# A third seven-product pair in the even gate/up blocks, and an order between the sums of weights and the first split of sums

## The chip, the core and the metric

The kernel runs on one core of one Trainium2 chip, in one launch. The metric is the device time of that launch in microseconds; lower is better. The engines are called as the profile calls them: PE is TensorE's matmul, PEld its weight load, DVE is VectorE, ACT is ScalarE, POOL is GpSimd, SP is SyncE, whose queue issues the loads of the weights.

## The reference

One decoder layer in float32 on 256 tokens of width 2048: a half-weighted SwiGLU feed-forward, a mixer (gated linear attention beside dilated attention, between one input and one output projection), and a second half-weighted SwiGLU feed-forward.

```python
D_MODEL = 2048; SEQ = 256; D_FF = 5632; FFN_RESIDUAL_WEIGHT = 0.5
...
def swiglu(x, w_gate, w_up, w_down):
    return (jax.nn.silu(x @ w_gate) * (x @ w_up)) @ w_down
...
x = x + FFN_RESIDUAL_WEIGHT * swiglu(rms_norm(x, ffn1_norm[l]), ffn1_w_gate[l], ffn1_w_up[l], ffn1_w_down[l])
h = rms_norm(x, mix_norm[l])
z = h @ w_in[l]
...
x = x + jnp.concatenate([o_g, o_a], axis=-1) @ w_out[l]
x = x + FFN_RESIDUAL_WEIGHT * swiglu(rms_norm(x, ffn2_norm[l]), ffn2_w_gate[l], ffn2_w_up[l], ffn2_w_down[l])
```

The change touches the gate and up products of both feed-forwards (2048 to 5632, twice), and through a shared helper the down product and the output projection.

## The kernel before

**Products.** Float32 operands are split into a high and a low part (`split`, lines 113 to 116: ScalarE copies the high part in the matmul type, VectorE subtracts it from the source), and a product takes three matmuls: high by high, weight-low by high, weight-high by low (`products`, lines 273 to 283). Activations are split once and stay in SBUF; weights are loaded and split as they are needed.

**Weights.** A load on SP's queue (line 221) brings one k-pair, 256 rows of k by two column groups of 512, 1 MB, into a raw buffer; there are three. The raw buffer holds four blocks of 512 columns. A plain pair is split in two parts, each 128 by 1,024, into a `wh` and a `wl` tile; there are four of each. `weights()` hands these parts to the matmuls in order and prepares the parts that come two later. A raw buffer is loaded again when the last instruction that reads it is done, a `wh`/`wl` pair is written again when the last matmul that reads it is done.

**Seven products.** A k-pair over both token halves and both column groups is a 2 by 2 by 2 block product: eight products of blocks, 24 matmuls. A "seven" pair takes seven products of sums of blocks (Strassen's way), 21 matmuls (`seven_products`, lines 293 to 317). The sums of activations are made once for the three pairs that can be sevens (`seven_forms`; `forms` holds pairs 0, 1 and 2 in both feed-forwards' gate/up stage). The sums of weights are made for every such pair on VectorE in `seven`, part "plain": line 243 writes two sums of 1,024 columns together, line 244 a third of 512, line 247 the fourth of 512 out of the third. Four parts go to the matmuls: "plain" (two blocks of the raw buffer), "last" (one block), "sums" (the first two sums), "more" (the third and fourth). In the gate/up stage the sums lie in a room of their own in `xs`, so the raw buffer is free after the splits of "plain" and "last" and line 247; in the down stage and the output projection the third and fourth sum are written back into the raw buffer.

**Gate/up blocks.** Each feed-forward has 11 blocks of 512 columns of gate and 512 of up, eight k-pairs each. `FF_ORDERS` (line 46) writes out their order; `g` is a seven, `s` a plain pair. Block 0 is all plain; blocks 1, 3, 5, 7 and 9 are `ssgsggss`, blocks 2, 4, 6, 8 and 10 `ssgssgss`. `seven_pair` runs a block: four banks collect the plain products and four more the products that belong to several outputs; after the last seven `fold` (lines 488 to 493) brings these to VectorE's side, and `evac` (lines 451 to 473) adds them, applies the silu gate and sends the result through transposes and moves on POOL's queue.

**Down stage.** `DOWN_ORDERS` (line 47) has sevens as well, with the same `seven`.

**Order.** The kernel is traced as a program; a planner then orders each engine's queue by a simulated time, taking what is ready and, among that, what is earlier in the program. Each engine works its queue strictly in that order on the chip. So an instruction whose operand comes later than planned holds up what stands behind it. `tc.issue_after(ins)` puts each instruction that is traced inside it on `ins`'s engine behind `ins` in that engine's order; on other engines it has no effect.

Of the kernel before, what the change touches and what calls it, by code (L numbers as in the profile page):

```python
# [28 lines left out]
EPS = 1e-6  # L29
WBUF = 4  # L30
FF_SEVEN = range(1, 11)
FF_THREE = range(1, 10, 2)
TAIL = 4
WARM = 10
GH, GDK, GDV, RANK = 4, 128, 256, 16
# [4 lines left out]
def _order(text):  # L40

    seven, plain = iter(range(text.count("g"))), iter(range(text.count("g"), len(text)))
    return [(next(seven), True) if c == "g" else (next(plain), False) for c in text]


FF_ORDERS = [_order("ssgsggss" if b in FF_THREE else "ssgssgss" if b in FF_SEVEN else "ssssssss") for b in range(FF // 512)]
DOWN_ORDERS = [_order("ssssssgssgssgsgsgsgsss"), _order("sgsgsgsgsgsgsgssgsssss")]
# [3 lines left out]
def layer_kernel(tc, x, xT, gains, gla_gate_up, gla_gate_bias, gla_out_norm, att_q_norm, att_k_norm,  # L51
                 w_ff1, w_dn1, w_mix, w_low, w_out, w_ff2, w_dn2, c_sq, c_rope, c_mask, out):

    nc = tc.nc
# [3 lines left out]
    with ExitStack() as es:  # L58
# [54 lines left out]
        def split(dst_h, dst_l, src):  # L113

            nc.scalar.activation(dst_h, src, AF.Copy)  # L115
            nc.vector.tensor_sub(dst_l, src, dst_h.bitcast(F32))  # L116
# [71 lines left out]

        AHEAD = 2
        ready = []  # L190
        raws = [None]
        started = []

        def wtile(name):
            return wp.tile([P, 2, 512], F32R, name=name, tag=name, bufs=WBUF)

        def prepare():
# [15 lines left out]
            if k in ("last", "sums", "more"):  # L213
                return seven(k, w)
# [7 lines left out]
            if k == "plain":  # L222
                return seven(k, w)
# [11 lines left out]
        def seven(part, w):  # L235

            raw = raws[0].bitcast(F32)
            room = rooms["gate" if w is w_ff1 or w is w_ff2 else "down"]
            blocks = raw.rearrange("p k j f -> p (k j) f")
            more = room.get("more", blocks[:, 0::3, :])  # L240
            if part == "plain":
                b1 = blocks[:, 0, :].unsqueeze(1).to_broadcast([P, 2, 512])
                nc.vector.tensor_add(room["sum"], b1, blocks[:, 1:3, :])  # L243
                nc.vector.tensor_add(more[:, 0, :], room["sum"][:, 0, :], blocks[:, 2, :])
                if "more" not in room:
                    split(room["wh"][:, 0, :], room["wl"][:, 0, :], blocks[:, 3, :])
                nc.vector.tensor_add(more[:, 1, :], more[:, 0, :], blocks[:, 3, :])  # L247
                wh, wl = wtile("wh"), wtile("wl")
                split(wh, wl, blocks[:, 1:3, :])
            elif part == "last":  # L250
                wh, wl = room["wh"], room["wl"]
                if "more" in room:
                    split(wh[:, 0, :], wl[:, 0, :], blocks[:, 3, :])
            else:
                wh, wl = wtile("wh"), wtile("wl")
                split(wh, wl, room["sum"] if part == "sums" else more)
            ready.append((wh, wl))

        def weights(early=False):
# [740 lines left out]
```

## Time and profile before

| | us |
|---|---|
| median of 3 runs | 1711.49 |
| lowest, highest | 1710.02, 1712.36 |
| the profiled execution, its own time | 1710.49 |
| its span, first to last instruction | 1708.7 |
| gate/up of feed-forward 1 | about 6 to 448 |
| its down stage | about 448 to 650 |
| mixer and output projection | about 650 to 1050 |
| feed-forward 2 | about 1050 to the end |

The profile is of one execution. Times in its rows count from the first instruction. A row of a group gives its count, its busy time and mean, then the idle time of its engine just before it and what ended that; a row of the timeline gives start, length, engine, line, what is written and read, shape, count, and in brackets the idle time before it with what ended it. Records of matmuls are longer than the distance between two of them, because matmuls are pipelined.

### The profile page before, as it was taken

The page shows a single profiled execution, that of the slowest core. Times are in us where ns is not written, and L with a number is a line of the kernel's source. Part 1 is how long each engine was busy: PE and PEld are TensorE (multiplying, and loading weights), DVE is VectorE, ACT ScalarE, POOL GpSimd, SP SyncE. Part 2 cuts the span into 40 slices and gives each one's busy share as a digit, 9 for nine tenths or more (in the row PEclk, how much of TensorE's full clock was granted, in tenths as well). Part 3 has the DMA queues.
Part 4 walks back from the last instruction along what each step waited for, and adds up shares of the span by engine and source line. Part 5 has one row for each costly group of instructions (what it writes and reads, how often), then busy time and mean ns, then how long its engine had stood idle before and what let it go on. Part 6 is the DMA issues. An engine that isn't in the chain of part 4 may idle for free.

```text
span 1708.7 us, 22402 instructions
## 1 busy us (share of the span) xinstructions
PE 1696.9 (99%) x7932; PEld 1477.4 (86%) x7932; DVE 1472.8 (86%) x1823; ACT 973.4 (57%) x1207; POOL 506.2 (30%) x1002
## 2 busy tenths in 40 slices
PE   9999999999999999999999999999999999999999
PEld 7888888888888878888888888888888888888887
DVE  6989999999899997577856688989998999899986
ACT  7656565555555555564654555556555655555553
POOL 0333334343400601064250034333333333420000
PEclk9999999999999999999999999999999999999999
DMA  8566656666666666567564457666666666666663
GB/s 347 211 232 225 218 210 236 212 235 216 235 245 223 216 220 226 195 231 243 190 217 169 151 198 249 231 234 210 235 224 229 223 215 219 222 247 232 220 235 135
DMA packets 85809, 378.63 MB, mean 222 GB/s; under 512 B 21393, under 2 KB 38801, under 8 KB 42689
## 3 DMA queue, kind: packets, MB, share of 16 engines
q1 hardware_dynamic: 50864, 350.25, 57.9%
q0 software_dynamic: 34112, 25.88, 5.4%
q8 instruction: 62, 1.02, 0.2%
q10 hardware_dynamic: 720, 1.07, 0.2%
q14 instruction: 51, 0.41, 0.1%
HBM read 354.57 MB, written 4.19 MB: 210 GB/s over the span
## 4 chain that ended last, share of the span: by engine, by line
PE 89%; DVE 5%; DMA 4%; issue 1%; POOL 0%; ACT 0%; DVEq 0%; SPq 0%; ACTq 0%; POOLq 0%
PE acc L281 19%; PE acc L283 19%; PE acc L279 19%; PE acc L305 5%; PE acc L306 5%; PE acc L304 5%; PE tp L283 4%; PE tp L281 4%; PE tp L279 4%; DVE wl L116 3%; DMA raw<-in_w_dn_dram 2%; PE tp L306 1%; PE tp L305 1%; PE tp L304 1%; DMA xs<-us 1%
## 5 line engine op out<-in xcount | busy, mean ns | idle before, releaser
L115 ACT ACTIVATE wh<-raw 128x1024 fp32r<-128x1024 f32 (+2 forms) x610 | 631.9, 1047 | 444.0 <-PE acc L283 207.0
L116 DVE TENSOR_TENSOR wl<-raw,wh 128x1024 fp32r<-128x1024 f32 (+1 forms) x608 | 733.1, 1215 | 127.0 <-ACT wh L115 124.3
L137 POOL DMA_DIRECT2D xs<-us x704 | 344.5, 497 | 545.6 <-DVE us L130 284.1
L283 PE MATMUL acc<-wh,hl 128*128 128x512 f32 x1192 | 359.3, 381 | 0.0
L281 PE MATMUL acc<-wl,hh 128*128 128x512 f32 x1192 | 358.8, 381 | 0.1
L279 PE MATMUL acc<-wh,hh 128*128 128x512 f32 x1192 | 347.9, 381 | 2.3 <-ACT wh L115 2.3
L279 PEld LDWEIGHTS acc<-wh,hh 128*128 128x128 f32 x1192 | 224.8, 189 | 35.4 <-ACT wh L115 3.5
L281 PEld LDWEIGHTS acc<-wl,hh 128*128 128x128 f32 x1192 | 225.1, 189 | 32.7 <-DVE wl L116 0.5
L283 PEld LDWEIGHTS acc<-wh,hl 128*128 128x128 f32 x1192 | 225.3, 189 | 32.2 <-issue 0.5
L115 ACT ACTIVATE wh<-xs 128x1024 fp32r<-128x1024 f32 x100 | 105.6, 1056 | 103.3 <-DVE xs L247 31.9
L116 DVE TENSOR_TENSOR wl<-xs,wh 128x1024 fp32r<-128x1024 f32 x100 | 120.4, 1214 | 2.7 <-ACT wh L115 2.6
L281 PE MATMUL acc<-wl,uh 128*128 128x512 f32 x368 | 113.1, 381 | 2.6 <-DVE wl L116 2.6
L283 PE MATMUL acc<-wh,ul 128*128 128x512 f32 x368 | 112.2, 379 | 0.0
L279 PE MATMUL acc<-wh,uh 128*128 128x512 f32 x368 | 106.2, 380 | 0.5 <-ACT wh L115 0.5
L137 POOL DMA_DIRECT2D hh<-us x128 | 62.1, 500 | 121.1 <-DVE xs L531 68.5
L243 DVE TENSOR_TENSOR xs<-raw 128x1024 f32<-128x1024 f32 x50 | 61.1, 1222 | 29.3 <-DMA raw<-in_w_ff_dram 29.2
L281 PEld LDWEIGHTS acc<-wl,uh 128*128 128x128 f32 x368 | 68.7, 189 | 15.1 <-DVE wl L116 5.6
L279 PEld LDWEIGHTS acc<-wh,uh 128*128 128x128 f32 x368 | 69.3, 189 | 11.1 <-ACT wh L115 1.3
L283 PEld LDWEIGHTS acc<-wh,ul 128*128 128x128 f32 x368 | 69.6, 189 | 9.9
L279 PE MATMUL tp<-wh,hh 128*128 128x512 f32 x200 | 61.6, 379 | 0.0
L281 PE MATMUL tp<-wl,hh 128*128 128x512 f32 x200 | 59.5, 379 | 0.0
L283 PE MATMUL tp<-wh,hl 128*128 128x512 f32 x200 | 59.5, 379 | 0.0
(326 smaller groups left out, 2540.0 us busy)
## 6 DMA issues: line engine op xcount, KB each, us to landing
raw<-in_w_ff_dram SPq DMA_DIRECT2D x175, 1024.0 KB, 5.1
raw<-in_w_dn_dram SPq DMA_DIRECT2D x88, 1024.0 KB, 4.9
raw<-in_w_mix_dram SPq DMA_DIRECT2D x48, 1024.0 KB, 5.0
raw<-in_w_out_dram SPq DMA_DIRECT2D x16, 1024.0 KB, 4.8
xs<-us POOLq DMA_DIRECT2D x704, 16.0 KB, 4.0
xs<-in_x_dram SPq DMA_DIRECT2D x2, 1024.0 KB, 9.5
xs<-in_x_dram POOLq DMA_DIRECT2D x2, 1024.0 KB, 5.9
hh<-us POOLq DMA_DIRECT2D x128, 16.0 KB, 3.7
```

Source lines behind the costliest of these rows:

```text
L115: nc.scalar.activation(dst_h, src, AF.Copy)
L116: nc.vector.tensor_sub(dst_l, src, dst_h.bitcast(F32))
L137: nc.gpsimd.dma_start(dst[32 * q:32 * q + 32, ..., r * n:(r + 1) * n], src[32 * r:32 * r + 32, ..., q * n:(q + 1) * n])
L243: nc.vector.tensor_add(room["sum"], b1, blocks[:, 1:3, :])
L279: nc.tensor.matmul(ps[j], lhsT=sh, rhs=alt(wh[:, j, :]), start=first and i == 0, stop=False)
L281: nc.tensor.matmul(ps[j], lhsT=sh, rhs=alt(wl[:, j, :]), start=False, stop=False)
L283: nc.tensor.matmul(ps[j], lhsT=sl, rhs=alt(wh[:, j, :]), start=False, stop=last and i == len(ws) - 1)
L304: nc.tensor.matmul(bank, lhsT=a[0], rhs=alt(ws[0][:, j, :]), start=start, stop=False)
L305: nc.tensor.matmul(bank, lhsT=a[0], rhs=alt(ws[1][:, j, :]), start=False, stop=False)
L306: nc.tensor.matmul(bank, lhsT=a[1], rhs=alt(ws[0][:, j, :]), start=False, stop=stop)
```

## The change

The list of blocks with three sevens goes from 1, 3, 5, 7, 9 to 1 to 9, so blocks 2, 4, 6 and 8 also take `ssgsggss`; block 10 keeps two. The instruction of line 247 is kept in `raws[1]`, and the split of the parts "sums" and "more" is traced inside `tc.issue_after` of it. Its subtract on VectorE then stands behind line 247 in VectorE's order; its copy on ScalarE is not bound. "more" reads what line 247 writes and comes after it in any case; "sums" does not.

```diff
 FF_SEVEN = range(1, 11)
-FF_THREE = range(1, 10, 2)
+FF_THREE = range(1, 10)
...
-        raws = [None]
+        raws = [None, None]
...
-                nc.vector.tensor_add(more[:, 1, :], more[:, 0, :], blocks[:, 3, :])
+                raws[1] = nc.vector.tensor_add(more[:, 1, :], more[:, 0, :], blocks[:, 3, :])
                 wh, wl = wtile("wh"), wtile("wl")
                 split(wh, wl, blocks[:, 1:3, :])
...
             else:
                 wh, wl = wtile("wh"), wtile("wl")
-                split(wh, wl, room["sum"] if part == "sums" else more)
+                with tc.issue_after(raws[1].ins):
+                    split(wh, wl, room["sum"] if part == "sums" else more)
             ready.append((wh, wl))
```

## The prediction

> **What bounds the kernel now.** The page's first part comes first, then a few pieces of the chain of work that ended last.
>
> ```profile
> span 1708.7 us, 22402 instructions
> PE 1696.9 (99%) x7932; PEld 1477.4 (86%) x7932; DVE 1472.8 (86%) x1823; ACT 973.4 (57%) x1207; POOL 506.2 (30%) x1002
> ```
> ```profile
> 110.78 0.86 PE acc L279 x4
> 111.64 0.22 PE acc L281
> ```
>
> TensorE is busy for all but 12 us, and four 512-column matmuls follow each other in 0.86 us, 0.215 us each. A matmul less is 0.215 us less, as long as TensorE's operands keep coming. Who delivers them shows in busy time by window, each from the first seven's `L243` of one gate/up block to that of the next (window, length, then busy us and count of PE, PEld, DVE, ACT, POOL, then clock, DMA share, GB/s). The windows are blocks 3 to 6.
>
> ```profile
> 128.53:168.00 39.47, 39.47 (x184) 34.59 (x183) 39.01 (x44) 24.56 (x28) 15.65 (x32) 1.00 0.64 223
> 168.00:208.40 40.40, 40.40 (x188) 35.16 (x187) 35.30 (x40) 22.07 (x26) 15.66 (x32) 1.00 0.66 225
> 208.40:248.00 39.60, 39.60 (x185) 34.69 (x184) 39.02 (x44) 24.68 (x28) 15.65 (x32) 1.00 0.63 224
> 248.00:288.00 40.00, 40.00 (x187) 35.01 (x187) 35.29 (x39) 22.02 (x25) 15.65 (x32) 1.00 0.65 226
> ```
>
> TensorE has no hole in any of them. VectorE alternates: 39.0 us of work in the 39.5 us of a block with three sevens, 35.3 us in one with two. The change makes every window of blocks 2 to 9 one of the first kind. So the stage moves from "TensorE alone" to "both engines, 0.45 us apart", and the question is what VectorE loses at the seams.
>
> **The reserve.** How far VectorE runs ahead is the distance from the end of a split's subtract to the first matmul that reads its `wl`. The first two rows are the full distance, just before block 3 (VectorE, then TensorE); the other two the tightest place of block 3, the last sums of its third seven.
>
> ```profile
> 126.79 1.23 DVE L116 TENSOR_TENSOR wl<-raw,wh 128x1024 fp32r<-128x1024 f32 x1 [0.76 <-ACT wh L115]
> 133.71 0.59 PE L281 MATMUL acc<-wl,hh 128*128 128x512 f32 x2
> ...
> 157.21 1.22 DVE L116 TENSOR_TENSOR wl<-xs,wh 128x1024 fp32r<-128x1024 f32 x1
> 159.61 0.38 PE L305 MATMUL acc<-wl,uh 128*128 128x512 f32 x1
> ```
>
> 128.02 to 133.71 is 5.7 us, all that four buffers hold; 158.43 to 159.61 is 1.2 us. A three-seven block eats 4.5 us of reserve in its middle, and its last two plain pairs give it back. What is left over is 1.2 us.
>
> **The seam.** The first seven's `L243` stands in VectorE's queue ahead of the second pair's splits and waits for its weights:
>
> ```profile
> 128.53 1.23 DVE L243 TENSOR_TENSOR xs<-raw 128x1024 f32<-128x1024 f32 x1 [0.51 <-DMA raw<-in_w_ff_dram]
> ...
> 164.09 1.21 DVE L492 TENSOR_TENSOR xs<-xs,acc 128x1024 f32<-128x1024 f32 x1
> 165.22 2.35 DVE L116 TENSOR_TENSOR wl<-raw,wh 128x1024 fp32r<-128x1024 f32 x2
> 170.25 1.23 DVE L243 TENSOR_TENSOR xs<-raw 128x1024 f32<-128x1024 f32 x1 [2.68 <-DMA raw<-in_w_ff_dram]
> ...
> 408.14 1.23 DVE L243 TENSOR_TENSOR xs<-raw 128x1024 f32<-128x1024 f32 x1 [1.42 <-DMA raw<-in_w_ff_dram]
> ```
> ```profile
> 167.79 1.06 ACT L115 ACTIVATE wh<-raw 128x1024 fp32r<-128x1024 f32 x1 [1.53 <-PE tp L283]
> ```
>
> After a two-seven block the wait is 0.51 us; after a three-seven one 2.68 us (block 4) and 1.42 us (block 10). Not all is loss: VectorE was as far ahead as the buffers let it, ScalarE got its next buffer from TensorE only at 167.79, so the next subtract could not have begun before 168.9. Of block 4's wait 1.35 us is real, of block 10's about 0.1 us. Middle: 0.7 us a seam, against 0.45 us of spare a block.
>
> **The change, part by part.** *Removed:* a plain pair is 24 matmuls (two k-tiles, two token halves, two column halves, three products each), a seven 21. Four blocks, two FFNs, one pair each: 8 x 3 = 24 matmuls, 24 x 0.215 = **-5.2 us**, all on the path while TensorE has no hole.
>
> By the Trainium skill, "TensorE: Matmul & The Clock Gate", section Back-to-back issue gap, a sustained stream of 512-column matmuls runs at about 131 ns each, which would make this 3.1 us and the whole sum below -2.7, so 1708.8 (estimates from that page). The chain's row says 215 ns over thousands of them, which the page has as the gap of a single matmul; the measurement decides.
>
> *Added:* each new seven brings three sums and 1,536 columns of split more.
>
> ```profile
> L243 DVE TENSOR_TENSOR xs<-raw 128x1024 f32<-128x1024 f32 x50 | 61.1, 1222 | 29.3 <-DMA raw<-in_w_ff_dram 29.2
> L247 DVE TENSOR_TENSOR xs<-xs,raw 128x512 f32<-128x512 f32 x50 | 34.2, 684 | 0.1
> L116 DVE TENSOR_TENSOR swl<-raw,swh 128x512 fp32r<-128x512 f32 x50 | 34.2, 684 | 0.0
> ```
>
> Neighbours overlap by some 0.08 us (165.22 x2 in 2.35), so 1,024 columns cost 1.14 and 512 cost 0.60 us: sums 1.14 + 0.60 + 0.60, splits 3 x 1.14 + 0.60, less the 2.28 of a plain pair, is 4.1 us. The windows show less, 39.0 - 35.3 = 3.7, their borders being uneven. All of it lies beside TensorE. ScalarE takes 1.6 us more in a window where it has 15 us free; POOL issues the same moves; SP issues one load a pair as before. The cover is the 0.45 us of spare and the 1.2 us of reserve. A seam that loses 0.7 us costs 0.25 us net a block; 16 seams make 4 us, of which the reserve and the two-seven block 10 take about half: **+2.0 us** (bounds 0, and the first rivals' prices).
>
> *The order edge in gate/up.* In the even blocks' first seven the first sums' split runs ahead of the fourth sum, as here in block 4:
>
> ```profile
> 179.67 0.67 DVE L244 TENSOR_TENSOR xs<-xs,raw 128x512 f32<-128x512 f32 x1
> 180.26 1.21 DVE L116 TENSOR_TENSOR wl<-xs,wh 128x1024 fp32r<-128x1024 f32 x1
> 181.39 0.69 DVE L247 TENSOR_TENSOR xs<-xs,raw 128x512 f32<-128x512 f32 x1
> ```
>
> `L247` is the last reader of that pair's raw buffer, so the swap frees it 1.1 us sooner and the load behind it on SP's queue lands sooner; what is queued behind the held subtract on VectorE only trades places, and that `wl` comes 0.6 us later. I take 0 for this; it is part of why I do not charge the seams in full.
>
> *The edge in the down stage.* There the last split reads the raw buffer after `L247` wrote it, and TensorE stands waiting for it (FFN 1; TensorE, ScalarE, VectorE):
>
> ```profile
> 498.69 0.38 PE L306 MATMUL tp<-wh,hl 128*128 128x512 f32 x1
> 499.64 0.48 PE L304 MATMUL tp<-wh,hh 128*128 128x512 f32 x1 [0.57 <-ACT wh L115]
> 499.96 0.38 PE L304 MATMUL acc<-wh,uh 128*128 128x512 f32 x1
> 500.59 0.92 PE L279 MATMUL acc<-wh,uh 128*128 128x512 f32 x3 [0.25 <-ACT wh L115]
> ```
> ```profile
> 498.54 2.00 ACT L115 ACTIVATE wh<-raw 128x1024 fp32r<-128x1024 f32 x2 [4.93 <-DVE raw L247]
> ```
> ```profile
> 496.60 1.22 DVE L116 TENSOR_TENSOR wl<-urs,wh 128x1024 fp32r<-128x1024 f32 x1
> 497.73 0.68 DVE L247 TENSOR_TENSOR raw<-raw 128x512 f32<-128x512 f32 x1
> ...
> 616.76 1.22 DVE L116 TENSOR_TENSOR wl<-urs,wh 128x1024 fp32r<-128x1024 f32 x1
> 617.90 0.68 DVE L247 TENSOR_TENSOR raw<-raw 128x512 f32<-128x512 f32 x1
> 618.50 0.69 DVE L157 TENSOR_TENSOR hf<-hh,gT 128x512 f32<-128x512 f32 x1
> 619.79 1.23 DVE L116 TENSOR_TENSOR wl<-raw,wh 128x1024 fp32r<-128x1024 f32 x1 [0.60 <-ACT wh L115]
> ...
> 1529.97 1.21 DVE L116 TENSOR_TENSOR wl<-urs,wh 128x1024 fp32r<-128x1024 f32 x1
> 1531.10 0.68 DVE L247 TENSOR_TENSOR raw<-raw 128x512 f32<-128x512 f32 x1
> ```
>
> Start to start 0.95 and 0.63 instead of 0.215: 1.1 us lost at 499.64 and 500.59. With `L247` 1.13 us sooner both go. At 617 VectorE gets back its 0.60 us, and TensorE's next stop is VectorE's:
>
> ```profile
> 623.34 0.70 PE L281 MATMUL acc<-wl,uh 128*128 128x512 f32 x2 [0.53 <-DVE wl L116]
> ```
>
> FFN 2 has the first place again (1531.10); I put its stops at half of FFN 1's, 0.6 us. Together 2.3 us at most; at least 0, if the sums' own `wl`, now 0.6 us later, is what TensorE then waits for. I take two thirds, **-1.6 us**.
>
> **Sum.** -5.2 + 2.0 - 1.6 = -4.8 us. The profiled execution took 1710.49 us, 1.8 around its span of 1708.7, and would become 1705.7; the median shown is 1.0 above it, so **1706.7 us**. About 0.2% (3.4 us) is what a measurement here can tell from no change.
>
> **Rivals.** (1) *VectorE becomes the bound and eats the gain.* For: 39.0 of 39.5 us, and `L243` waits 29.2 us over the whole run. Against: those waits fall where VectorE is full ahead. At 0.25 to 0.7 us a block over 14 blocks (16 less the first of each FFN, which has the reserve) it is 3.5 to 9.8 us on -6.8: 1708.2 to 1714.5, middle 1710.5.
>
> The Trainium skill leans this way: "Perfetto Trace Analysis", Identifying the Most-Contended Engine, has TensorE judged by its weight loads, not by matmul occupancy; those are 86% here, like VectorE, and by that TensorE would not be alone at the bound. The 0.215 us spacing without holes speaks against it.
>
> (2) *Slower.* The order at the seam stays as it is and the waits stay whole: from `L243` of block 3 to that of block 4 it is 170.25 - 128.53 = 41.7 us, while a block of 183 matmuls needs 39.4. As VectorE falls behind, none of the wait is free any more: 1.9 (between 1.42 and 2.68) less 0.45 is 1.4 us a block, x 14 = 20 us, on -6.8: about 1725. It decides at 0.5 us of uncovered wait a block (even) and 0.73 (slower by 0.2%). Against: a subtract stands ahead of `L243` by right where its operand is ready, and a VectorE that lags has such work, so the order itself should give way.
>
> (3) *The edge does nothing in the down stage* (other work fills the place, or the stop moves to the next tile): -3.2, 1708.3.
>
> (4) *A matmul taken out is worth less than its spacing*, because neighbours overlap and something else paces them. The least that the page's first part allows is a weight load, 1477.4 us / 7932 = 0.186 us: -4.5 + 2.0 - 1.6 = -4.1, 1707.4. Against: no hole between matmuls in four windows. The 131 ns of the Trainium skill's TensorE page, above, would be the far end of this.
>
> **Chances.** Forecast 0.46, (1) 0.30, (2) 0.15, (3) 0.06, (4) 0.03. Of (3), which lies near the border, a third counts as faster, and (4) does. Faster 0.51, within 0.2% 0.34, slower 0.15. Range: with all gains and no new wait -7.5 (1704.0), with (1) at its dear end 1714.5; (2) is left out. I widen the low end by 0.5 us for the spread of the runs shown.
>
> **What would show it.** Right: 24 matmuls fewer; windows of even blocks with VectorE at 39 us and 39.5 us long; `L247` ahead of the sums' split everywhere; no stop of TensorE on `wl` between 90 and 450 us; the 499.64 stop gone. Wrong: stops of TensorE on `wl` or `wh` in blocks 3 to 9, growing block by block (2) or small in each (1); `L243` still waiting 1.4 us or more in every block; new stops in the down stage, whose order is written anew with every change ahead of it.

## The result, and the profile after

The changed kernel took 1728.22 us (median of 5 runs, 1724.79 to 1732.68) against 1711.49 us for the kernel before: a ratio of 1.010, 95% interval 1.009 to 1.011. It is slower by 17 us, where 4.8 us less had been forecast. Rival (2) of the prediction, whose time was about 1725, came nearest. The profiled execution has a span of 1730.8 us and is the slowest of the five (1732.68 us). The first part of its page:

```profile
span 1730.8 us, 22448 instructions
PE 1702.0 (98%) x7908; PEld 1472.0 (85%) x7908; DVE 1503.1 (87%) x1863; ACT 981.7 (57%) x1223; POOL 507.1 (29%) x1002
```

The 24 matmuls are gone (7932 to 7908), and yet TensorE's busy time went up, by 5 us: this row doesn't show where it stood still. The windows from seam to seam can (blocks 4, 5 and 6 of feed-forward 1; window, length, then PE, PEld, DVE, ACT, POOL, clock, DMA share, GB/s).

```profile
171.25:212.16 40.91, 39.67 (x183) 34.14 (x182) 39.18 (x44) 23.91 (x28) 15.64 (x32) 1.00 0.62 218
212.16:253.41 41.25, 40.36 (x187) 34.74 (x186) 39.20 (x45) 23.85 (x28) 15.63 (x32) 1.00 0.63 220
253.41:294.17 40.76, 39.55 (x182) 34.05 (x181) 39.19 (x44) 23.84 (x27) 15.66 (x32) 1.00 0.62 217
```

VectorE has the 39.2 us of work that the prediction gave it. But a block now takes 40.8 to 41.3 us and not 39.5. VectorE's timeline shows what comes on top of the 39.2, here at the seams of blocks 6 and 7:

```profile
253.41 1.23 DVE L243 TENSOR_TENSOR xs<-raw 128x1024 f32<-128x1024 f32 x1 [1.88 <-DMA raw<-in_w_ff_dram]
...
289.28 1.22 DVE L493 TENSOR_TENSOR xs<-xs,acc 128x1024 f32<-128x1024 f32 x1
290.41 2.36 DVE L116 TENSOR_TENSOR wl<-raw,wh 128x1024 fp32r<-128x1024 f32 x2
294.17 1.23 DVE L243 TENSOR_TENSOR xs<-raw 128x1024 f32<-128x1024 f32 x1 [1.40 <-DMA raw<-in_w_ff_dram]
```

At every seam from block 3 on the first seven's `L243` waits 1.4 to 2.1 us for its load (1.9 at most in feed-forward 1), and VectorE waits hardly anywhere else in these blocks: 39.2 of work and 1.5 of wait make nearly the whole block. The splits of the pair that TensorE needs next stand behind `L243`. The Trainium skill, "PSUM — Partial Sum Buffer", section Engine vs sequencer instructions, calls VectorE's queue strictly first in, first out. These rows agree: nothing passes `L243` in its 1.40 us.

TensorE itself doesn't stop at the seam; what VectorE loses there shows further on in the block. For the rest of this text a *stop* of TensorE is what the distance between the starts of two matmuls has over 0.216 us, summed over distances above 0.23 us. From the seam of block 2 to that of block 10 the stops of both feed-forwards make 21.1 us. Of these 6.4 us lie 17 us behind the seam, at the low part of the plain pair behind the first seven, in block 6 here:

```profile
270.07 0.70 PE L282 MATMUL acc<-wl,hh 128*128 128x512 f32 x2 [0.35 <-DVE wl L116]
```

The other 14.7 us lie 28 to 30 us behind the seam, in the third seven, at its last part "more". VectorE, ScalarE and TensorE in block 6:

```profile
276.44 1.22 DVE L243 TENSOR_TENSOR xs<-raw 128x1024 f32<-128x1024 f32 x1
277.57 1.22 DVE L116 TENSOR_TENSOR wl<-raw,wh 128x1024 fp32r<-128x1024 f32 x1
278.71 0.69 DVE L116 TENSOR_TENSOR swl<-raw,swh 128x512 fp32r<-128x512 f32 x1
279.31 0.68 DVE L244 TENSOR_TENSOR xs<-xs,raw 128x512 f32<-128x512 f32 x1
279.91 0.69 DVE L116 TENSOR_TENSOR ul<-xs,uh 128x512 fp32r<-128x512 f32 x1
280.51 0.68 DVE L247 TENSOR_TENSOR xs<-xs,raw 128x512 f32<-128x512 f32 x1
```
```profile
281.31 1.06 ACT L115 ACTIVATE wh<-xs 128x1024 fp32r<-128x1024 f32 x1 [1.96 <-DVE xs L247]
```
```profile
281.18 0.38 PE L307 MATMUL acc<-swh,hl 128*128 128x512 f32 x1
282.42 0.48 PE L305 MATMUL tp<-wh,uh 128*128 128x512 f32 x1 [0.86 <-ACT wh L115]
```

The fourth sum (`L247`) begins 4.1 us after `L243`, here and in most blocks; two splits of the raw buffer and one of activations stand ahead of it. ScalarE needs it for the high part of "more", and TensorE for the next matmul: start to start 1.24 us in place of 0.215. The view of waits has both waits, at the seam and for the fourth sum (first the rows of the kernel after, then one of before; us in all, times, longest):

```profile
DVE xs L243 <- DMA raw<-in_w_ff_dram: 31.8, 20, 3.3
ACT wh L115 <- DVE xs L247: 87.6, 45, 3.7
```
```profile
ACT wh L115 <- DVE xs L247: 31.9, 23, 1.7
```

`L243`'s total is hardly more than before's 29.2 us. What changed is what a microsecond of it costs, since VectorE is no longer ahead. Another wait shows that: a VectorE that is as far ahead as the buffers let it waits for ScalarE, which waits for TensorE to free a buffer. Between the seams of blocks 3 and 10 of feed-forward 1 the view has this row for the kernel before, and no such row for the kernel after:

```profile
DVE wl L116 <- ACT wh L115: 5.8, 7, 1.4
```

The stops by stage, in us, with the whole run's median and its ratio to the kernel before on the same chip:

| kernel | start, block 0 | gate/up 1 | down 1 | mixer | block 0 of FFN 2 | gate/up 2 | down 2 | median | ratio, 95% |
|---|---|---|---|---|---|---|---|---|---|
| before | 4.0 | 0.1 | 5.1 | 7.5 | 0.3 | 0.0 | 2.2 | 1711.49 | |
| after | 5.2 | 9.9 | 3.0 | 8.6 | 2.9 | 12.7 | 4.5 | 1728.22 | 1.009 to 1.011 |
| e1 no edge | 4.4 | 9.8 | 5.0 | 8.4 | 0.3 | 11.2 | 4.3 | 1727.42 | 1.0075 to 1.0105 |
| e2 edge alone | 4.0 | 0.8 | 2.2 | 7.6 | 0.3 | 0.7 | 1.7 | 1709.07 | 0.9974 to 0.9992 |
| e3 seam | 5.6 | 7.1 | 1.8 | 7.5 | 1.0 | 8.6 | 3.7 | 1720.34 | 1.0029 to 1.0066 |
| e4 seam, later | 4.3 | 7.2 | 4.1 | 7.5 | 0.3 | 7.9 | 5.5 | 1723.01 | 1.0047 to 1.0077 |
| e6 early sums | 3.8 | 6.7 | 2.6 | 7.6 | 0.3 | 5.0 | 5.0 | 1716.47 | 1.0017 to 1.0040 |
| e5 both | 3.2 | 1.9 | 2.7 | 8.4 | 0.3 | 0.6 | 4.6 | 1707.55 | 0.9967 to 0.9986 |
| e12 e5 again | 3.8 | 0.8 | 4.6 | 8.9 | 0.3 | 0.4 | 4.5 | 1709.07 | 0.9973 to 0.9990 |
| e11 both, two sevens | 3.4 | 0.5 | 3.3 | 7.5 | 0.3 | 0.8 | 1.6 | 1708.84 | 0.9975 to 0.9993 |
| e9 less in the shadow | 3.2 | 9.6 | 2.0 | 8.4 | 0.3 | 9.5 | 4.0 | 1723.24 | 1.0058 to 1.0093 |
| e10 less before it | 3.6 | 5.2 | 3.6 | 8.4 | 0.3 | 4.2 | 4.1 | 1715.21 | 1.0008 to 1.0027 |
| e13 code moved on | 1.2 | 1.6 | 3.6 | 8.4 | 0.4 | 2.5 | 2.6 | 1713.33 | 1.0006 to 1.0024 |
| e14 code left | 2.8 | 1.2 | 2.8 | 7.5 | 0.3 | 0.7 | 3.9 | 1706.06 | 0.9960 to 0.9981 |

The two profiled spans differ by 22.1 us. The rows make 22.3: 24 matmuls -5.2, the gate/up stages +9.7 and +12.7, the down stages -2.1 and +2.4, the start, the mixer and block 0 of feed-forward 2 +4.8. Of the last, 2.6 us are block 0, where VectorE waits once for a transfer of the residual (the stops there are 0.3 us in nearly every other run):

```profile
DVE xs L323 <- DMA resid<-xs: 4.6, 1, 4.6
```

### The profile page after: what moved, and what is told of

Its sections match the earlier page's. It is cut to its first block, busy times and chain, and to the rows that moved or that the text cites. A ratio compares the mean times of both kernels' runs of the same rounds, so it can differ in the third digit from the quotient of the medians.

```text
span 1730.8 us, 22448 instructions
## 1 busy us (share of the span) xinstructions
PE 1702.0 (98%) x7908; PEld 1472.0 (85%) x7908; DVE 1503.1 (87%) x1863; ACT 981.7 (57%) x1223; POOL 507.1 (29%) x1002
## 4 chain that ended last, share of the span: by engine, by line
PE 42%; DVE 22%; DMA 19%; issue 9%; POOL 5%; ACT 2%; DVEq 0%; ACTq 0%; SPq 0%; POOLq 0%
DVE wl L116 11%; PE acc L282 10%; PE acc L284 10%; PE acc L280 10%; DMA xs<-us 7%; DMA raw<-in_w_dn_dram 5%; POOL xs L137 4%; DMA raw<-in_w_ff_dram 3%; DMA hh<-us 3%; PE tp L284 2%; PE tp L282 2%; PE tp L280 2%; ACT wh L115 2%; PE acc L306 1%; PE acc L307 1%
## 5 line engine op out<-in xcount | busy, mean ns | idle before, releaser
L115 ACT ACTIVATE wh<-raw 128x1024 fp32r<-128x1024 f32 (+1 forms) x602 | 622.4, 1047 | 409.9 <-PE acc L284 196.6
L282 PE MATMUL acc<-wl,hh 128*128 128x512 f32 x1128 | 341.4, 382 | 5.9 <-DVE wl L116 5.8
L284 PE MATMUL acc<-wh,hl 128*128 128x512 f32 x1128 | 340.7, 382 | 0.0
L280 PE MATMUL acc<-wh,hh 128*128 128x512 f32 x1128 | 330.5, 382 | 2.0 <-ACT wh L115 2.0
L282 PEld LDWEIGHTS acc<-wl,hh 128*128 128x128 f32 x1128 | 212.0, 189 | 42.3 <-DVE wl L116 12.7
L280 PEld LDWEIGHTS acc<-wh,hh 128*128 128x128 f32 x1128 | 213.4, 190 | 33.8 <-ACT wh L115 2.7
L284 PEld LDWEIGHTS acc<-wh,hl 128*128 128x128 f32 x1128 | 213.5, 190 | 30.1 <-DVE hl L557 0.2
L115 ACT ACTIVATE wh<-xs 128x1024 fp32r<-128x1024 f32 x116 | 122.6, 1057 | 144.0 <-DVE xs L247 87.6
L116 DVE TENSOR_TENSOR wl<-xs,wh 128x1024 fp32r<-128x1024 f32 x116 | 141.4, 1221 | 3.3 <-ACT wh L115 1.7
L243 DVE TENSOR_TENSOR xs<-raw 128x1024 f32<-128x1024 f32 x58 | 70.9, 1222 | 31.9 <-DMA raw<-in_w_ff_dram 31.8
L457 ACT ACTIVATE sg<-sg,rt 128x512 f32<-128x512 f32 x40 | 28.9, 722 | 68.8 <-DVE sg L456 68.7
L306 PE MATMUL acc<-wl,hh 128*128 128x512 f32 x170 | 64.6, 380 | 0.4 <-DVE wl L116 0.4
```

What stands on the lines that cost most here:

```text
L280: nc.tensor.matmul(ps[j], lhsT=sh, rhs=alt(wh[:, j, :]), start=first and i == 0, stop=False)
L282: nc.tensor.matmul(ps[j], lhsT=sh, rhs=alt(wl[:, j, :]), start=False, stop=False)
L284: nc.tensor.matmul(ps[j], lhsT=sl, rhs=alt(wh[:, j, :]), start=False, stop=last and i == len(ws) - 1)
L306: nc.tensor.matmul(bank, lhsT=a[0], rhs=alt(ws[1][:, j, :]), start=False, stop=False)
L457: nc.scalar.activation(sg, sg, AF.Silu, scale=rt[:, t:t + 1])
```

## The experiments

**One part of the change at a time.** `e1_three_no_edge` keeps the new sevens and drops the order; `e2_edge_alone` keeps the order and drops the sevens.

```diff
-                with tc.issue_after(raws[1].ins):
-                    split(wh, wl, room["sum"] if part == "sums" else more)
+                split(wh, wl, room["sum"] if part == "sums" else more)
```
```diff
-FF_THREE = range(1, 10)
+FF_THREE = range(1, 10, 2)
```

> Three sevens in blocks 1 to 9, without the order edge. Theory A (the seam: the first seven's L243 stands ahead of the next pair's splits and waits for a load that is issued only when the last pair of the block before has been split, about 1.5 us in each block): the edge has no part in it, so L243 waits stay 1.4 to 2.7 us at each seam and the time stays at 1723 to 1733. Theory B (VectorE has too much work, wherever it stands): the same, 1723 to 1733. Theory C (the edge puts the fourth sum and what waits for it in a worse place): most of the loss goes, 1706 to 1713.

> The order edge with the old lists of blocks. Theories A and B: gate/up stays without stops of TensorE, the down stages move a little either way; 1708 to 1715. Theory C: slower by 5 us or more, above 1716.

`e1` took 1727.4 us, as the whole change did, and `e2` 1709.1, by the ratio 2.9 us less than before (interval 1.4 to 4.4). So the slowdown is that of the sevens. One part of theory A did not hold in `e1`: in feed-forward 1 `L243` waits only 0.85 to 0.95 us at six of the eight seams from block 3 on, and a block still takes 40.7 us. Without the edge the fourth sum of the third seven comes later, 5.9 us after the first sum in most blocks, and VectorE has a second wait there, for the high part of "more" (VectorE in block 7):

```profile
293.66 1.23 DVE L243 TENSOR_TENSOR xs<-raw 128x1024 f32<-128x1024 f32 x1 [0.95 <-DMA raw<-in_w_ff_dram]
...
315.26 1.23 DVE L243 TENSOR_TENSOR xs<-raw 128x1024 f32<-128x1024 f32 x1
...
321.17 0.69 DVE L247 TENSOR_TENSOR xs<-xs,raw 128x512 f32<-128x512 f32 x1
...
323.06 1.23 DVE L116 TENSOR_TENSOR wl<-xs,wh 128x1024 fp32r<-128x1024 f32 x1 [0.60 <-ACT wh L115]
```

So the seam's wait alone does not set the pace. The edge does what it was given: in `e2` the last split's place in the down stage reads (VectorE, then TensorE)

```profile
497.38 0.69 DVE L247 TENSOR_TENSOR raw<-raw 128x512 f32<-128x512 f32 x1
497.98 1.23 DVE L116 TENSOR_TENSOR wl<-urs,wh 128x1024 fp32r<-128x1024 f32 x1
```
```profile
498.62 0.38 PE L307 MATMUL acc<-wh,hl 128*128 128x512 f32 x1
499.30 0.48 PE L305 MATMUL tp<-wh,hh 128*128 128x512 f32 x1 [0.30 <-ACT wh L115]
499.62 0.38 PE L305 MATMUL acc<-wh,uh 128*128 128x512 f32 x1
```

with `L247` ahead of the sums' split. The stop there is 0.47 us, where before it was two of together 1.1; over both down stages the stops fall by 3.4 us, while the gate/up stages stop 1.4 us more.

**The seam.** If `L243`'s place in the queue is the cause, it has to be put back by hand. `e3_seam_one_split` holds the first seven's `L243` behind the subtract of the first part of the pair ahead of it in the order (`split` hands that subtract back); `e4_seam_two_splits` behind the second part's.

```diff
             for k in range(2):
                 ...
-                split(wh, wl, raws[0][:, k])
+                got = split(wh, wl, raws[0][:, k])
+                if k == 0:
+                    raws[2] = got
...
-                nc.vector.tensor_add(room["sum"], b1, blocks[:, 1:3, :])
+                if "more" in room and i % 8 == 0:
+                    with tc.issue_after(raws[2].ins):
+                        nc.vector.tensor_add(room["sum"], b1, blocks[:, 1:3, :])
+                else:
+                    nc.vector.tensor_add(room["sum"], b1, blocks[:, 1:3, :])
```

> The changed kernel, and the first seven's L243 of each gate/up block is put behind the subtract of the first part of the pair before it. Theory A: the wait at the seam falls from 1.5 to under 0.7 us, the distance from seam to seam from 40.8 to about 39.6 us, and 10 to 19 us come back: 1709 to 1718. Theory B: the wait shifts to another place of VectorE's queue or its work fills the time, above 1722. Theory C: no change, 1724 to 1732.

> As the run before, but behind the subtract of the second part too, so that L243 comes later by 1.1 us and the evacuation's first operations. Theory A: the wait at the seam is gone, 1706 to 1716, unless the first seven's sums now come too late for TensorE, which would show as stops at the third pair. Theory B: above 1722. Theory C: 1724 to 1732.

`e3` is 8 us faster than the change and still slower than before; `e4` is no better. Both miss theory A's ranges, and `e4` lies where theory B, too much work for VectorE, had it; the next pair of runs decides that. `L243`'s wait at the seam is gone (the other sevens' first sum is line 249 in `e3`; the seam's own, line 247, has no row of waits at all):

```profile
DVE xs L249 <- DMA raw<-in_w_ff_dram: 0.4, 1, 0.4
```

In its place VectorE waits there for ScalarE, so it is as far ahead again as the buffers let it (first the seam ahead of block 7, then the row of waits between the seams of blocks 3 and 10 of feed-forward 1):

```profile
292.55 1.23 DVE L116 TENSOR_TENSOR wl<-raw,wh 128x1024 fp32r<-128x1024 f32 x1 [0.98 <-ACT wh L115]
```
```profile
DVE wl L116 <- ACT wh L115: 8.2, 9, 1.0
```

But the third seven stops TensorE as before, with ScalarE's high part of "more" behind the fourth sum (line 253 here; VectorE, ScalarE, TensorE of block 6):

```profile
279.31 0.69 DVE L253 TENSOR_TENSOR xs<-xs,raw 128x512 f32<-128x512 f32 x1
```
```profile
280.11 1.06 ACT L115 ACTIVATE wh<-xs 128x1024 fp32r<-128x1024 f32 x1 [1.97 <-DVE xs L253]
```
```profile
281.23 0.48 PE L311 MATMUL tp<-wh,uh 128*128 128x512 f32 x1 [0.59 <-ACT wh L115]
```

A block takes 40.3 us there. The seam was one cause of two.

**The fourth sum.** `e6_early_sums_alone` holds, in the gate/up sevens, the split of "plain" behind the third sum and that of "last" behind the fourth, so that the sums come first; `e5_seam_and_early_sums` is that on top of `e3`.

```diff
-                nc.vector.tensor_add(more[:, 0, :], room["sum"][:, 0, :], blocks[:, 2, :])
+                third = nc.vector.tensor_add(more[:, 0, :], room["sum"][:, 0, :], blocks[:, 2, :])
...
-                split(wh, wl, blocks[:, 1:3, :])
+                if "more" in room:
+                    with tc.issue_after(third.ins):
+                        split(wh, wl, blocks[:, 1:3, :])
+                else:
+                    split(wh, wl, blocks[:, 1:3, :])
...
-                    split(wh[:, 0, :], wl[:, 0, :], blocks[:, 3, :])
+                    with tc.issue_after(raws[1].ins):
+                        split(wh[:, 0, :], wl[:, 0, :], blocks[:, 3, :])
```

> The kernel with the first seven's L243 behind one split, and in every gate/up seven also: the subtract of part plain behind the third sum, that of part last behind the fourth. Theory A2 (two places of VectorE's order cost: the wait at the seam, and in the third seven the fourth sum, which stands behind three other subtracts while TensorE waits for the high part of the split made of it): the stops at the third seven, about 1.1 us a block, go, the distance from seam to seam falls from 40.3 to 39.5 us, 1703 to 1711. Theory B (VectorE has too much work wherever it stands): 1717 or more.

> The changed kernel with the early sums of the run before but with the seam as it was. If the seam alone sets the pace (theory A: seam to seam is VectorE's work up to the last split of the block plus the load behind it), the pace stays at 40.5 to 41 us and the stops of TensorE only change place: 1722 to 1731. If the late fourth sum is what costs (theory D), the stops go and it is 1707 to 1714.

Early sums alone take 12 us off the change; 1716.47 us lies between the two ranges of the expectation, so neither the seam alone nor the late fourth sum alone was the cause. Both together take off 20.7: 1707.55 us, below the kernel before. In `e5` the third seven has its fourth sum (line 253) 3.0 us after the first (line 249), ahead of `swl` and the sums' split; block 6, then the windows of blocks 7 and 8:

```profile
271.13 1.22 DVE L249 TENSOR_TENSOR xs<-raw 128x1024 f32<-128x1024 f32 x1
272.38 0.69 DVE L250 TENSOR_TENSOR xs<-xs,raw 128x512 f32<-128x512 f32 x1
272.99 1.22 DVE L116 TENSOR_TENSOR wl<-raw,wh 128x1024 fp32r<-128x1024 f32 x1
274.13 0.68 DVE L253 TENSOR_TENSOR xs<-xs,raw 128x512 f32<-128x512 f32 x1
274.73 0.68 DVE L116 TENSOR_TENSOR swl<-raw,swh 128x512 fp32r<-128x512 f32 x1
```
```profile
288.92:328.44 39.52, 39.52 (x185) 34.46 (x184) 39.10 (x45) 24.52 (x29) 15.64 (x32) 1.00 0.64 227
328.44:367.96 39.52, 39.52 (x185) 34.46 (x184) 39.10 (x45) 24.53 (x29) 15.65 (x32) 1.00 0.64 226
```

VectorE does the same 39.1 us of work in 39.52 us and TensorE has no hole. So it was neither the amount of VectorE's work nor the loads that bound the gate/up stages of the changed kernel, but the order of VectorE's queue.

**Less work for VectorE, order left.** To tell amount from place in another way, two kernels leave out most columns of an add of `fold`, about 1 us of VectorE a block: `e9_less_work_in_the_shadow` of the last add (line 493), just ahead of the seam, `e10_less_work_before_it` of the two before it (491, 492).

```diff
-    nc.vector.tensor_add(v4(t4[:, 1::2, :]), v4(t4[:, 1:3, :]),
-                         m[1].unsqueeze(1).to_broadcast([P, 2, 2, 256]))
+    nc.vector.tensor_add(v4(t4[:, 1::2, :])[:, :, :, 0:16], v4(t4[:, 1:3, :])[:, :, :, 0:16],
+                         m[1][:, :, 0:16].unsqueeze(1).to_broadcast([P, 2, 2, 16]))
```
```diff
-    nc.vector.tensor_add(u1, p1, m[2]),
-    nc.vector.tensor_add(u2, u1, m[3]),
+    nc.vector.tensor_add(u1[:, :, 0:16], p1[:, :, 0:16], m[2][:, :, 0:16]),
+    nc.vector.tensor_add(u2[:, :, 0:16], u1[:, :, 0:16], m[3][:, :, 0:16]),
```

> The changed kernel with the fold's last addition (L493) cut to 16 of each 256 columns; the rest of its result is left as it was. It stands behind the last split of the block, in the time in which the load for the next first seven is under way. Theory A: the wait of L243 grows by what is left out, from 1.5 to about 2.4 us, the pace of 40.8 us and the time do not move, 1723 to 1732. Theory B: 0.9 us a block come back, 1709 to 1717.

> The changed kernel with the fold's two additions L491 and L492 cut to 16 of each 256 columns, the rest of their results left out; they stand ahead of the block's last split. Theory A and theory B both: about 0.9 us a block less, the pace 39.9 us, the wait of L243 as it was, 1710 to 1718. Against the run before it this tells whether it is the amount of VectorE's work or its place.

A late window of each, `e9` first, and under it a seam of `e9`:

```profile
332.94:373.69 40.75, 39.88 (x184) 34.42 (x183) 38.28 (x45) 23.87 (x28) 15.62 (x32) 1.00 0.62 219
```
```profile
330.03:369.66 39.63, 39.63 (x185) 34.46 (x184) 38.19 (x44) 24.21 (x28) 15.64 (x32) 1.00 0.64 225
```
```profile
292.19 1.23 DVE L243 TENSOR_TENSOR xs<-raw 128x1024 f32<-128x1024 f32 x1 [1.80 <-DMA raw<-in_w_ff_dram]
```

In `e9` VectorE has 0.9 us less to do and the block is as long as in the change: what is cut ahead of the wait is waited instead (1.7 to 2.3 us at all but one of its seams from block 3 on). In `e10` the block of this window shrinks to 39.6; from the seam of block 2 to that of block 10 the mean is 40.1 us, against 40.8 in `e9` and 40.9 in the change. In the whole `e9` is 5 us faster than the change, with intervals that overlap. This pair is weaker than `e5`, because the planner also gave `e10` an earlier fourth sum; how much of its gain is order and how much is work stays open.

**Are the 24 matmuls worth their 5.2 us once the order is right?** `e11_all_edges_two_sevens` has all edges of `e5` with the old list of blocks; `e12_e5_again` ran `e5` beside it.

```diff
-FF_THREE = range(1, 10)
+FF_THREE = range(1, 10, 2)
```

> All the order edges of e5_seam_and_early_sums, but the list of three-seven blocks as before the change (odd blocks only), so TensorE has 7932 matmuls again. It takes apart what the edges bring and what the 24 matmuls bring. Theory: with the order right a matmul taken out is worth its spacing, so this kernel is 24 x 0.215 = 5.2 us slower than e5's in the same batch, less whatever e5 still loses in gate/up (2.0 us of stops in its trace): 3 to 5 us slower, around 1711. Rival: e5 gains nothing from the matmuls because VectorE, at 39.2 of 39.5 us, gives it back elsewhere, and e5's gain is the edge in the down stage alone (e2: 1709.1): then within 1 us of e5's, 1707 to 1708.

> The kernel of e5_seam_and_early_sums again, beside e11_all_edges_two_sevens on the same chip. Both theories: 1707.6, between 1705.9 and 1710.1; the difference to e11 decides between them.

In gate/up they are: from the seam of block 2 to that of block 10 a block takes 39.81 and 39.85 us (feed-forward 1 and 2) in `e11`, 39.52 and 39.47 in `e12`, which makes 5.4 us in 16 blocks (by the trace of `e5`, the same kernel as `e12`, 3.9). In the whole they are not: 1708.84 and 1709.07 us, as the rival had it. In the table `e12` stops for 1.3 us more in the first down stage, 1.4 in the mixer and 2.9 in the second down stage; `e5` stops 0.6 us less than `e11` in the first of these, 0.9 more in the mixer and 3.0 more in the second down stage, so the last alone is steady. Through both down stages VectorE and ScalarE have the same order in the two kernels. What differs in the second is a load (number 321 of the loads of weights on SP's queue, counted from 0; a seven's first sum waits for it). A window around it with its queues, `e12`, then `e11`, and the VectorE row that waits for it in each:

```profile
q8 instruction: 1, 0.02, 0.9%
issues: line engine op xcount, KB each, median us to landing
raw<-in_w_dn_dram SPq DMA_DIRECT2D x1, 1024.0 KB, 6.2
```
```profile
raw<-in_w_dn_dram SPq DMA_DIRECT2D x1, 1024.0 KB, 4.8
```
```profile
1639.15 1.23 DVE L249 TENSOR_TENSOR urs<-raw 128x1024 f32<-128x1024 f32 x1 [2.89 <-DMA raw<-in_w_dn_dram]
```
```profile
1638.66 1.22 DVE L249 TENSOR_TENSOR urs<-raw 128x1024 f32<-128x1024 f32 x1 [1.44 <-DMA raw<-in_w_dn_dram]
```

In `e12` a 16 kB packet of instruction code falls into the load, and it lands 1.4 us later. The same holds in all nine traces with 7908 matmuls, for this load (5.6 to 6.2 us after its issue ends, against 4.5 in the three with 7932) and for number 293 (6.0 to 6.5 against 4.8 to 5.1); and all nine stop for 3.7 to 5.5 us in the second down stage, the three for 1.6 to 2.2. These are two loads picked out of 332. In all fourteen traces, those of the next two runs among them, 83 loads have a packet in at least three traces and none in at least three others: the median of their differences is 0.2 us, and 16 of them differ by 1 us or more.

**Moving the code.** If the packets are the cause, 24 matmul records more ahead of all work should move them back. `e13_code_moved_on` has 13 more warm-up matmuls on zeros, `e14_code_left` one more, both of 64 columns in place of 128 (the diff is `e13`'s; `e14` has `WARM + 1`).

```diff
-        for _ in range(WARM):
-            nc.tensor.matmul(wb[:, :P], lhsT=warm[:, :P], rhs=warm[:, :P], start=True, stop=True)
+        for _ in range(WARM + 13):
+            nc.tensor.matmul(wb[:, :64], lhsT=warm[:, :P], rhs=warm[:, :64], start=True, stop=True)
```

> e12_e5_again with 23 first matmuls on zeros of 64 columns in place of 10 of 128 (a float32 matmul has two records). It has the same order on every engine as e14_code_left, with 24 matmul records more ahead of all work, as many as the change took out. What is left out or changed of the result: nothing. Question: why do the down stage and the mixer of e12 stop 5.6 us more in its trace than those of e11, when nothing in them was edited? Theory: the 16 kB packets of instruction code come once in 128 matmuls and their weight loads; with 24 matmuls fewer they come later against the work, and in all nine traces with 7908 matmuls one falls into the loads numbered 293 and 321 (1.2 us after e12's issue), which land 1.0 to 1.9 us later than in the three with 7932. With 24 records more ahead they leave both loads again: 293 lands in 5.0 to 5.1 us and 321 in 4.5, feed-forward 2's down stage stops for 1.6 to 2.5 us in place of 4.5, and the whole is 2 to 3 us faster than e14. Rival: the down stage takes back by its own pace what the stage ahead gains (a TensorE that comes earlier waits longer for VectorE): then both loads land as in e12, or land sooner and the stops stay at 4 us or more; no difference to e14.

> The control for e13_code_moved_on: 11 first matmuls of 64 columns, the same order on every engine, the code packets where e12 has them to within two matmuls. Both theories: loads 293 and 321 land in about 6.1 and 5.9 us, feed-forward 2's down stage stops for 4 to 5 us, 1708 to 1709.5 in all. The theory of the code packets has it 2 to 3 us slower than e13, the rival has the two the same.

`e13` took 1713.33 us (ratio 1.0006 to 1.0024) and `e14` 1706.06 (0.9960 to 0.9981): 7 us apart, the other way round than the theory had it. Two assumptions in the expectation failed. The order is not the same on every engine: it differs up to 93 us, in the mixer and in block 0 of feed-forward 2, though not from there to the end. And the warm-up was thought to end before the first weights come; it doesn't (`e13`, then `e14`):

```profile
1.49 10.08 PE L104 MATMUL tp<-warm 128*128 128x64 f32 x46 [1.49 <-DVE warm L101]
```
```profile
1.49 4.95 PE L104 MATMUL tp<-warm 128*128 128x64 f32 x22 [1.49 <-DVE warm L101]
```

That costs 5.1 us at the start, of which 1.6 come back as shorter stops in block 0. In the second down stage, whose order the two share, the theory holds in direction: loads 293 and 321 land in 4.8 and 5.2 us in `e13`, without the packet, and in 6.2 and 6.1 in `e14`, with it; the stops are 2.6 and 3.9 us. The 5.2 us are not the 4.5 that were expected: in `e13` the packet falls early into the load ahead, number 320, which lands in 5.7 us there and in 4.4 to 4.6 in the other thirteen traces. And `e13` stops 3.9 us more than `e14` in the two gate/up stages, the first down stage and the mixer. So it is shown that the packet makes these loads late; that it is what takes back the 24 matmuls' 5.2 us is not shown.

## Why the prediction was wrong

- **The matmuls, -5.2.** Right in count and, in gate/up with a mended order, in size (`e12` against `e11`: 5.4 us; `e5` against `e11`: 3.9). In the change itself TensorE never got to use them.
- **VectorE's cost beside TensorE, +2.0: the step that failed.** The windows for it were right (39.2 us of work, 39.5 of room). The 0.7 us a seam was wrong. It took the middle between a seam whose wait was half free and one whose wait was free, and both belonged to a VectorE that was a full four buffers ahead. With every block a three-seven block it doesn't get that far ahead again, and each seam's 1.4 to 2.1 us counts whole: in place of +2.0 us the gate/up stages stop 22.4 us more, the loss of the next point included. Rival (2) had said just this; it was given 0.15 because "a subtract stands ahead of `L243` by right where its operand is ready, and a VectorE that lags has such work, so the order itself should give way". The order is fixed ahead of the run from simulated times, and it did not give way: the splits stood behind `L243` at every seam. The price of rival (2), 1.4 us a block over 14 blocks, met the size: the mean from the seam of block 2 to that of block 10 in both feed-forwards, 40.87 us a block, less 39.5 is 1.4 us a block. That the size fits so well is partly luck: with the seam mended only 8 to 9 us came back (`e3`), not 20.
- **What no rival named.** In `e3` the seam is mended and 8 of the some 20 us come back. The rest hangs on the fourth sum: 3.0 us after the first in the third seven of block 3 before (`L243` at 151.28, `L247` at 154.27), 4.1 us after it in the change. The prediction's 1.2 us of reserve at that very place was measured on the old order, and on the low part. What ran short is the high part, which ScalarE makes of the fourth sum; in block 3 before it was ready 1.5 us ahead of its first matmul (ScalarE, then TensorE):

```profile
155.07 1.06 ACT L115 ACTIVATE wh<-xs 128x1024 fp32r<-128x1024 f32 x1
157.66 0.38 PE L304 MATMUL acc<-wh,uh 128*128 128x512 f32 x1
```

- **The two places together.** Mending them one by one nearly adds up (by the ratios to the kernel before: seam alone 9, early sums alone 12, both 21 us), but that doesn't split the loss cleanly by place. Early sums also shorten the seam's wait: at the seams of blocks 4 to 10 of both feed-forwards it falls from 21.9 us in all to 16.4 in `e6`.
- **The edge in gate/up, 0.** Right within what can be told, 1728.2 with it and 1727.4 without, but two effects stand behind the 0: with the edge the fourth sum of the third seven comes 4.1 us after the first and not 5.9, and the seam's wait is longer.
- **The edge in the down stage, -1.6.** Right in sign and mechanism and somewhat small: -2.9 (-4.4 to -1.4) in `e2`. In the change the stops of the first down stage fall (from 5.1 to 3.0 us), those of the second rise (from 2.2 to 4.5); the late loads are part of that (load 321 lands there in 5.7 us).
- **The rivals by their marks.** Of the marks given for "wrong", two came true as written: `L243` waits 1.4 us or more in every block from 3 on, and TensorE stops in blocks 3 to 9. They don't grow block by block: once the reserve is gone every block loses about the same. One slip in the sums: the middle of rival (1), 1708.2 to 1714.5, is 1711.4 and not 1710.5; nothing else hangs on it.
- **Left open.** Why the planner puts `L243` and `L247` where it does; whether a fourth raw buffer, which might bring the load sooner, would mend the seam too, which wasn't tried; and what in the mixer and the first down stage takes its part of the 5.4 us back in `e12`. Of the kernels that keep the new sevens, `e14` is the fastest at 1706.06 us, but its interval overlaps those of `e5` and `e12`, and those of `e2` and `e11`, which do without them. What is shown is that mending the order makes the sevens harmless; that they pay is not.

## What to carry to other kernels

A wait in an engine's queue is free only as long as that engine is ahead: when a change brings it to within a per cent of the engine that sets the pace, every wait in its queue is to be priced whole, at the place where it stands, and an order written out ahead of the run is to be taken as it is. Where the work fits and the time doesn't come, look for the one instruction that waits at the head of a queue, and after mending it look again, for the next late one was hidden behind it. And compare stage by stage: in `e12` 5.4 us gained in one kind of stage were lost in three others, and the total alone would have said that the gain never existed.

## What the runs showed of the hardware

- **Instruction code takes part in the DMA traffic.** The queue q8 on the page, by its count that of TensorE's code, moves 62 packets of 16 kB; 7908 matmuls and as many weight loads by 62 is 255 instructions a packet. The Trainium skill, "Runtime: NRT & Kernel Launch", section Instruction fetch mechanics, has blocks of 16 KiB or 256 instructions, and crossing a boundary mostly hidden. The count agrees. Hidden it is not in every load: loads 293 and 321 land 1.0 to 1.9 us later with the packet in them, though the median over 83 loads is 0.2 us. Taking out 24 matmuls put packets into these two loads, and 24 more records ahead of them took the packets out again (`e13`).
- **A small float32 matmul hardly gets shorter with its columns.** The warm-up on 64 columns took 10.08 us for 46 records, 0.219 us each; with 128 columns 20 records took 4.64 us, 0.232 each (`e12`). Narrowing them saved next to nothing, and the 12 matmuls that `e13` has more than `e14` took 5.1 us.
- **Work removed just ahead of a wait was worth nothing to the block:** 0.9 us a block less on VectorE, which sets the pace there, left the block at 40.8 us (`e9`).
